# The compression's projections, blocks and first layer inside the loop of the recurrence

## The chip, the cores and the metric

The kernel runs on one core of a Trainium2 chip. A core has TensorE (matrix products, PE in the profile, with its weight loads as PEld), VectorE (DVE), ScalarE (ACT), GpSimd (POOL) and SyncE (SP, which here issues every DMA). Each engine takes its instructions in the order in which the program issues them. The metric is device microseconds of one execution.

## The reference

A decoder layer over 512 tokens of width 1024. After a norm, one wide product gives queries, keys and values of an attention, the input and gate of a recurrence (RG-LRU) and two merge gates. The parts that matter here are the compression of keys and values (blocks of 32 tokens through a two-layer network) and the recurrence:

```python
h = _rmsnorm(x, norm1_g)
proj = h @ w_in
# compression of keys and of values
blocks = jnp.concatenate([chunks[:, :-1], chunks[:, 1:]], axis=2) + pos[None, None, :, None, :]
hid = jax.nn.gelu(jnp.einsum('bnlgd,ldf->bngf', blocks, w1) + b1)
return jnp.einsum('bngf,fd->bngd', hid, w2) + b2
# recurrence
xc = conv(xb) + conv_b                       # 4 taps over time, per channel
r = sigmoid(xr @ wa + ba); i = sigmoid(xr @ wi + bi)   # 16 diagonal blocks
log_a = -LRU_C * r * softplus(-lam)
a = exp(log_a); b = sqrt(-expm1(2 * log_a)) * (i * xc)
h[t] = a[t] * h[t-1] + b[t]                  # scan over time
return h * gelu(gate)
```

Attention over compressed, selected and windowed keys follows, then the merge of both branches, an output product and a SwiGLU network with a residual.

## The kernel before

All products are float32 in three passes: each operand is split into a high half (float32r) and a low half (the rest), and `mm3` (L193) adds high by high, high by low and low by high. Weights come in the order of `weight_chunks` (L65) as chunks of 512 KB. `Weights.get(key, k, ahead)` (L174) hands out the next chunk after it has *cut* all chunks up to `ahead` further on, which are issued on ScalarE (the high half, L164) and VectorE (the low half, L167), and has issued the loads of two more on SP (L143). The raw chunks have two buffers, so a load waits until the chunk two before it has been cut. Cuts stand in the queues of ScalarE and VectorE where `get` is called: what is issued before them runs before them.

The recurrence's channels are 8 groups of 128. After the norm and the first group, the loop `for c in range(2, 8)` (L418) makes one turn for each group: the gate's projection of group c (`proj_cm`, 24 matmuls of 512 columns), `lru_coeffs(c-2)` (sigmoids and tanh on ScalarE, two operations on GpSimd, five products on VectorE), `lru_conv(c-1)` (a copy on ScalarE, the four taps on VectorE), the input's projection, `lru_parts(c-1)` (its split: `xch` on ScalarE, `xcl` on VectorE) and `lru_gates(c-1)` (six matmuls against diagonal blocks, which need both halves). The projections use four PSUM banks called dense, the gates two called s; two called t take transposes.

Behind the loop come, in this order: the four projections of the compression's keys and values, mixed with the rest of groups 6 and 7; `kv_evac` (four copies each that lay an accumulator out by pairs of tokens); and a loop over six of the sixteen merge gates (L550) that carries the rest. In this second loop stand the block additions `blocks_add` (GpSimd, L475), their split `blocks_split` (L186, L187), the first layer's eight weight chunks with 12 matmuls of 256 columns each (*hidden*), the roots `lru_roots` (ScalarE, L546), the product with the root and the scan `lru_scan` (GpSimd L379, VectorE L381), the gates' GELU (L575), `lru_out` (GpSimd L385 and a store), and at its end `hidden_gelu` (VectorE and ScalarE) and the memsets of the attention's tiles. In the second loop `get` is called with `ahead=2`. Key, query and value projections follow, where the halves of weights alternate between GpSimd and VectorE, then attention and the network.

The program's own list of what stands in a turn of the second loop:

```python
        for n in w1_after(c):
            kv, cc = divmod(n, 4)
            wh, wl = W.get(("w1", "cmp_w1_" + "kv"[kv], cc), 4, ahead=int(n in (7, w1_after(c)[-1])))
...
        W.cut(W.used + 1)
        W.load(W.used + 3)
        if c == 0:
            lru_roots(2, 4, 6)
```

Of the kernel before, what the change touches and what calls it, by code (L numbers as in the profile page):

```python
# [59 lines left out]
def w1_after(c):  # L60

    return [c] if c < 4 else [2 * c - 4, 2 * c - 3]


def weight_chunks():  # L65
# [34 lines left out]
def hybrid_block_kernel(ctx: ExitStack, tc: tile.TileContext, x: bass.AP, wpk: bass.AP,  # L100
# [257 lines left out]

    def lru_coeffs(c):
# [18 lines left out]
    def lru_scan(c):  # L378
        pool.tensor_tensor(out=tv[:, c, :], in0=tv[:, c, :], in1=mv[:, c, :], op=OP.mult)  # L379
        hs = live[c] = lt()  # L380
        dve.tensor_tensor_scan(hs, av[:, c, :], tv[:, c, :], 0.0, op0=OP.mult, op1=OP.add)  # L381

    def lru_out(c):
        lr = lt()
        pool.tensor_tensor(out=lr, in0=live.pop(c), in1=gg[:, c, :], op=OP.mult)  # L385
        nc.sync.dma_start(lru_d[c], lr)
# [31 lines left out]
    for c in range(2, 8):  # L418
        accg = proj_cm(cm("w_in", C_LRUG + P * c), ahead=1)
        lru_coeffs(c - 2)  # L420
        lru_conv(c - 1, accx)
        accx = proj_cm(cm("w_in", C_LRUX + P * c), ahead=1)
        lru_parts(c - 1)
        lru_gates(c - 1)
        act.copy(gg[:, c, :], accg)
        if c == 3:
            pool.iota(dm, pattern=[[-1, 512]], base=384, channel_multiplier=1,
                      allow_small_or_imprecise_dtypes=True)
            pool.iota(cd, pattern=[[P, NT], [-16, 32]], base=-31, channel_multiplier=1,
                      allow_small_or_imprecise_dtypes=True)  # L430
            pool.tensor_scalar(valid, cd[:, :, 0], 0.0, None, op0=OP.is_ge)
            for d in (dm, cd.rearrange("p t n -> p (t n)")):
                far = lt(n=d.shape[1])
                pool.tensor_scalar(far, d, 0.0, BIG, op0=OP.is_lt, op1=OP.mult)
                pool.tensor_tensor(out=d, in0=d, in1=far, op=OP.add)
# [13 lines left out]

    w2 = W.get(("w2",), 4, ahead=2)  # L450
    acck = [proj_cm(cm("w_in", 1024), ahead=2)]
    lru_conv(7, accx)
    lru_coeffs(6)
    lru_parts(7)
    acck.append(proj_cm(cm("w_in", 1024 + P), ahead=2))
    kv_evac(0, acck[0], act.copy)
    acck.append(proj_cm(cm("w_in", 1024 + 2 * P), ahead=2))
    lru_gates(7)
    lru_coeffs(7)
    kv_evac(1, acck[1], act.copy)  # L460

# [10 lines left out]
    def blocks_add(kv, v):  # L472
# [4 lines left out]
                           in1=pos[:, :, None, None].to_broadcast([P, 8, NKV, NCMP]), op=OP.add)  # L477

# [59 lines left out]
    blocks_add(0, 0)  # L538
    blocks_split(0, 0)
    blocks_add(0, 1)  # L540
    acck.append(proj_cm(cm("w_in", 1024 + 3 * P), ahead=2))
    kv_evac(2, acck[2], dve.tensor_copy)

    def lru_roots(*cs):
        for c in cs:
            act.activation(mv[:, c:c + 2, :], mv[:, c:c + 2, :], AF.Sqrt, scale=-4.0)  # L546

    lru_roots(0)
    acc = None
    for c in range(N_EARLY):  # L550
        prev, acc = acc, proj_cm(cm("w_in", C_MERGE + P * c), ahead=2)
        if c:
            merge_gate(c - 1, bc2, prev, bufs=1)
        if c == 0:
            kv_evac(3, acck[3], dve.tensor_copy)
            blocks_split(0, 1)
        if c in (2, 4):
            blocks_split(1, c // 2 - 1)
        for n in w1_after(c):
            kv, cc = divmod(n, 4)  # L560
            wh, wl = W.get(("w1", "cmp_w1_" + "kv"[kv], cc), 4, ahead=int(n in (7, w1_after(c)[-1])))
            if cc == 0:
                hid[kv] = bank("s")[:, :256]
            for jj in range(4):
                mm3(hid[kv], [m[:, 4 * (n % 2) + jj, :] for m in blk[kv, cc // 2]],
                    [w[:, jj, :] for w in (wh, wl)], cc == 0 and jj == 0, cc == 3 and jj == 3)
        W.cut(W.used + 1)
        W.load(W.used + 3)
        if c == 0:
            lru_roots(2, 4, 6)  # L570
        if c in (1, 3):
            blocks_add(1, c // 2)
        if c in (1, 2):
            for j in (4 * c - 4, 4 * c - 2):
                act.activation(gg[:, j:j + 2, :], gg[:, j:j + 2, :], AF.Gelu_apprx_tanh)  # L575
        if c > 1:
            lru_out(2 * c - 4)
            lru_out(2 * c - 3)
        if c < 4:
            lru_scan(2 * c)  # L580
            lru_scan(2 * c + 1)
        if c == 5:
            merge_gate(5, bc2, acc, bufs=1)
            hxt = bc.tile([P, 512], F32, tag="hx", name="hx", bufs=1)
            hxs = [hidden_gelu(kv, hid[kv]) for kv in range(2)]
            lru_es.close()
            vpool, v_es = open_pool(name="vpool", bufs=1)
            kpool, k_es = open_pool(name="kpool", bufs=16)
            vst = vpool.tile([P, 2, NT, NKV, P], F32R, name="vst")
# [4 lines left out]
            for m in (vcx, *kpad):  # L594
                pool.memset(f(m), 0.0)
# [699 lines left out]
```

## Time and profile before

| | us |
|---|---|
| median of 3 runs | 1012.44 (1012.0 to 1012.83) |
| the profiled execution | 1012.1 |
| its span, first to last instruction | 1010.0 |
| TensorE busy | 981.0 (97%) |
| VectorE busy | 570.5 (56%) |
| ScalarE busy | 458.6 (45%) |
| GpSimd busy | 223.1 (22%) |

The profile is one execution. Times in rows are microseconds from the start of the span unless marked ns. A busy share is an average over the whole span; the stretches of the region at hand say more. In rows of the timeline the first two numbers are the start and the duration, and what stands in brackets is how long the engine stood idle before the instruction and what ended it. A matmul's duration contains time that overlaps its neighbours, so that matmuls in a row are counted by their starts. Tile names are the program's: whi and wlo are the halves of a weight chunk, hth and htl those of the normed input, lt a tile of the recurrence's ring buffer, tv, av and mv its terms, decays and roots, shifted and blkh/blkl the compression's blocks.

### The profile page before, as it was taken

To read this page: it belongs to the slowest core of one execution; us is meant where nothing else is said; L and a number is where in the kernel's file an instruction comes from. 1 tells how busy PE (TensorE), PEld (TensorE's weight loads), DVE (VectorE), ACT (ScalarE), POOL (GpSimd) and SP (SyncE) were. 2 spreads that over 40 slices of the span, in tenths; PEclk is the share of its full clock that TensorE was granted. 3 is DMA by queue.
4 is the path that set the end of the run, shared out by engine and by line. 5 is a ranking of instruction groups with operands and counts; after the bars stand their busy time and mean duration, and the time that the engine had idled before them with its cause. 6 is when DMAs were issued, how large, how long until landed. Compare 5 with 4: busy or idle time off the path is not lost.

```text
span 1010.0 us, 13183 instructions
## 1 busy us (share of the span) xinstructions
PE 981.0 (97%) x4915; PEld 817.0 (81%) x4915; DVE 570.5 (56%) x1053; ACT 458.6 (45%) x867; POOL 223.1 (22%) x271
## 2 busy tenths in 40 slices
PE   6999997799999999999999999999999999999998
PEld 5878876588898888778888888988888888888887
DVE  5777679746766787887875544623322332231311
ACT  6544565336545777776773334523222322231210
POOL 1031148713201555645542002200000000000000
PEclk9999999999999999999999999999999999999999
DMA  5322324642213111322113464132332233232401
GB/s 190 105 84 83 123 84 138 196 148 92 90 56 116 63 53 43 105 84 64 33 63 99 151 254 132 45 122 84 88 119 86 83 92 117 84 125 63 167 21 42
DMA packets 32175, 100.65 MB, mean 100 GB/s; under 512 B 3696, under 2 KB 4080, under 8 KB 32112
## 3 DMA queue, kind: packets, MB, share of 16 engines
q1 hardware_dynamic: 32112, 99.82, 30.7%
q8 instruction: 38, 0.62, 0.2%
q14 instruction: 25, 0.20, 0.1%
HBM read 91.42 MB, written 8.39 MB: 99 GB/s over the span
## 4 chain that ended last, share of the span: by engine, by line
PE 86%; DVE 7%; ACT 3%; issue 2%; DMA 2%; POOL 0%; ACTq 0%; DVEq 0%
PE ps_b L197 14%; PE ps_b L198 14%; PE ps_b L196 14%; PE ps_dense L1006 9%; PE ps_dense L198 5%; PE ps_dense L197 5%; PE ps_dense L196 5%; PE ps_t L880 3%; PE ps_s L197 2%; PE ps_s L196 2%; PE ps_s L198 2%; DVE wlo L167 2%; PE ps_s L849 2%; PE ps_s L850 2%; PE ps_pv L908 2%
## 5 line engine op out<-in xcount | busy, mean ns | idle before, releaser
L167 DVE TENSOR_TENSOR wlo<-raw,whi 128x1024 fp32r<-128x1024 f32 (+2 forms) x199 | 193.6, 989 | 114.0 <-ACT whi L164 113.6
L164 ACT CAST whi<-raw 128x1024 fp32r<-128x1024 f32 (+2 forms) x207 | 166.0, 819 | 136.8 <-PE ps_b L198 69.1
L196 PE MATMUL ps_b<-h2h,whi 128*128 128x512 f32 (+1 forms) x376 | 143.4, 381 | 0.0
L198 PE MATMUL ps_b<-h2h,wlo 128*128 128x512 f32 (+1 forms) x376 | 143.2, 381 | 0.0
L197 PE MATMUL ps_b<-h2l,whi 128*128 128x512 f32 (+1 forms) x376 | 143.2, 381 | 0.0
L198 PE MATMUL ps_dense<-hth,wlo 128*128 128x512 f32 (+1 forms) x232 | 87.9, 379 | 11.2 <-DVE wlo L167 11.2
L871 POOL TENSOR_SCALAR p<-p,st,gates 128x128 f32<-128x128 f32 (+3 forms) x128 | 80.0, 638 | 84.7 <-DVE st L867 47.2
L1205 DVE TENSOR_TENSOR sg<-sg,ps_b 128x512 f32<-128x512 f32 x22 | 15.2, 689 | 138.2 <-PE ps_b L198 138.2
L196 PE MATMUL ps_dense<-hth,whi 128*128 128x512 f32 (+1 forms) x232 | 87.4, 377 | 0.0
L197 PE MATMUL ps_dense<-htl,whi 128*128 128x512 f32 (+1 forms) x232 | 87.1, 375 | 0.0
L197 PEld LDWEIGHTS ps_b<-h2l,whi 128*128 128x128 f32 x376 | 70.7, 188 | 15.0
L196 PEld LDWEIGHTS ps_b<-h2h,whi 128*128 128x128 f32 x376 | 70.7, 188 | 14.9
L198 PEld LDWEIGHTS ps_b<-h2h,wlo 128*128 128x128 f32 x376 | 70.7, 188 | 14.8
L861 ACT ACTIVATE p<-p,st 128x128 f32<-128x128 f32 (+3 forms) x128 | 72.0, 563 | 23.0 <-DVE st L856 22.3
L197 PE MATMUL ps_b<-wlo,gh 128*128 128x512 f32 (+1 forms) x198 | 73.2, 370 | 0.0
L198 PE MATMUL ps_b<-whi,gl 128*128 128x512 f32 (+1 forms) x198 | 73.1, 369 | 0.0
L196 PE MATMUL ps_b<-whi,gh 128*128 128x512 f32 (+1 forms) x198 | 73.1, 369 | 0.0
L186 ACT CAST gh<-sg 128x512 fp32r<-128x512 f32 x22 | 13.6, 620 | 123.2 <-DVE sg L1205 123.2
L892 DVE TENSOR_TENSOR ptl<-ps_t,pth 128x512 fp32r<-128x512 f32 x80 | 55.1, 689 | 21.1 <-ACT pth L886 20.4
L856 DVE CUSTOM_DVE_ANT_0 p<-ps_s,bias 128x128 f32<-128x128 f32 (+3 forms) x128 | 61.2, 482 | 9.2 <-PE ps_s L850 6.2
L198 PEld LDWEIGHTS ps_dense<-hth,wlo 128*128 128x128 f32 x232 | 44.4, 191 | 21.7 <-DVE wlo L167 13.5
L886 ACT CAST pth<-ps_t 128x512 fp32r<-128x512 f32 x80 | 46.5, 582 | 29.7 <-PE ps_t L880 29.2
(265 smaller groups left out, 2072.8 us busy)
## 6 DMA issues: line engine op xcount, KB each, us to landing
raw<-in_wpk_dram SPq DMA_DIRECT2D x150, 512.0 KB, 3.6
mg_d<-mt SPq DMA_DIRECT2D x16, 256.0 KB, 4.3
mt<-mg_d SPq DMA_DIRECT2D x16, 256.0 KB, 3.0
xt<-in_x_dram SPq DMA_DIRECT2D x4, 512.0 KB, 5.6
lru_d<-lt SPq DMA_DIRECT2D x8, 256.0 KB, 5.6
lraw<-lru_d SPq DMA_DIRECT2D x8, 256.0 KB, 2.7
x<-in_x_dram SPq DMA_DIRECT2D x4, 512.0 KB, 6.5
out_dram<-o SPq DMA_DIRECT2D x7, 256.0 KB, 2.0
```

Source lines behind the costliest of these rows:

```text
L164: (on_hi or act.copy)(hi[:, sl], raw[:, sl])
L167: eng.tensor_tensor(out=lo[:, sl], in0=raw[:, sl], in1=f(hi[:, sl]), op=OP.subtract)
L196: pe.matmul(acc, lhsT=ah, rhs=bh, start=start, stop=False)
L197: pe.matmul(acc, lhsT=ah, rhs=bl, start=False, stop=False)
L198: pe.matmul(acc, lhsT=al, rhs=bh, start=False, stop=stop)
L856: dve.tensor_tensor_reduce(out=p, in0=accs.pop((h, br, t)), in1=bias[h][:, 384 - t * P:512], scale=-1.0, scalar=3e38, op0=OP.add, op1=OP.m ...
L861: act.activation(p, p, AF.Exp, bias=stat[h][:, 0, br, t:t + 1], scale=-1.0, accum_out=stat[h][:, 1, br, t:t + 1])
L871: pool.tensor_scalar(p, p, sm[:, t:t + 1], gates[:, t, c:c + 1], op0=OP.mult, op1=OP.mult)
L880: pe.transpose(pt[:, o_:o_ + P], probs[h, br, t][:, k * P:(k + 1) * P], ident)
L886: act.copy(ph, pts[h, gi][0])
L892: dve.tensor_tensor(out=pl, in0=pt, in1=f(ph), op=OP.subtract)
L1006: pe.matmul(acc, lhsT=a[l], rhs=b[r], start=start and i == 0, stop=stop and i == 2)
```

## The change

The compression's four projections move into turns 2 to 5 of the first loop, behind the gates of the turn; their copies follow one turn later, all on ScalarE. The block additions stand in turns 4 to 7, their splits at the end of the same turns, and the first layer's eight chunks go by twos into turns 5, 6, 7 and behind the first merge projection. The weights' order in memory follows. The roots of groups 0 and 1 are taken in turn 4, of 2 and 3 in turn 6, the rest behind the loop, and the scans of groups 0, 1 and 2 stand in turns 5, 6 and 7; a scan's result goes over the roots instead of into the ring buffer. The rest of groups 6 and 7, five scans, the GELUs and the outputs are spread over the six merge projections, where `get` now has `ahead=1` and the extra cuts and loads are gone. The first layer's accumulators use the banks t instead of s. The pools of the compression open ahead of the loop.

```diff
-def w1_after(c):
-    return [c] if c < 4 else [2 * c - 4, 2 * c - 3]
+W1_AFTER = {5: (0, 1), 6: (2, 3), 7: (4, 5), 8: (6, 7)}
...
-    for c in range(2, 8):
-        L += [cm("w_in", C_LRUG + P * c), cm("w_in", C_LRUX + P * c)]
-    L += [("w2",)]
-    L += [cm("w_in", 1024 + P * c) for c in range(4)]
-    for c in range(N_EARLY):
+    for c in range(2, 9):
+        if c < 8:
+            L += [cm("w_in", C_LRUG + P * c), cm("w_in", C_LRUX + P * c)]
+        else:
+            L += [("w2",), cm("w_in", C_MERGE)]
+        if c < 6:
+            L += [cm("w_in", 1024 + P * (c - 2))]
+        L += [("w1", "cmp_w1_" + "kv"[j // 4], j % 4) for j in W1_AFTER.get(c, ())]
+    for c in range(1, N_EARLY):
         L += [cm("w_in", C_MERGE + P * c)]
-        L += [("w1", "cmp_w1_" + "kv"[j // 4], j % 4) for j in w1_after(c)]
...
     def lru_scan(c):
         pool.tensor_tensor(out=tv[:, c, :], in0=tv[:, c, :], in1=mv[:, c, :], op=OP.mult)
-        hs = live[c] = lt()
-        dve.tensor_tensor_scan(hs, av[:, c, :], tv[:, c, :], 0.0, op0=OP.mult, op1=OP.add)
+        dve.tensor_tensor_scan(mv[:, c, :], av[:, c, :], tv[:, c, :], 0.0, op0=OP.mult, op1=OP.add)
...
+    def hidden(n):
+        kv, cc = divmod(n, 4)
+        wh, wl = W.get(("w1", "cmp_w1_" + "kv"[kv], cc), 4, ahead=1)
+        if cc == 0:
+            hid[kv] = bank("t")[:, :256]
+        for jj in range(4):
+            mm3(hid[kv], [m[:, 4 * (n % 2) + jj, :] for m in blk[kv, cc // 2]],
+                [w[:, jj, :] for w in (wh, wl)], cc == 0 and jj == 0, cc == 3 and jj == 3)
...
     for c in range(2, 8):
         accg = proj_cm(cm("w_in", C_LRUG + P * c), ahead=1)
         lru_coeffs(c - 2)
         lru_conv(c - 1, accx)
+        if c in (4, 6):
+            lru_roots(c - 4)
+        if c >= 5:
+            lru_scan(c - 5)
         accx = proj_cm(cm("w_in", C_LRUX + P * c), ahead=1)
         lru_parts(c - 1)
+        if 3 <= c < 7:
+            kv_evac(c - 3, acck.pop(c - 3), act.copy)
         lru_gates(c - 1)
         act.copy(gg[:, c, :], accg)
+        if c >= 4:
+            blocks_add(*divmod(c - 4, 2))
+        if c < 6:
+            acck[c - 2] = proj_cm(cm("w_in", 1024 + P * (c - 2)), ahead=1)
+        for n in W1_AFTER.get(c, ()):
+            hidden(n)
+        if c >= 4:
+            blocks_split(*divmod(c - 4, 2))
...
+    w2 = W.get(("w2",), 4, ahead=1)
     acc = None
     for c in range(N_EARLY):
-        prev, acc = acc, proj_cm(cm("w_in", C_MERGE + P * c), ahead=2)
+        prev, acc = acc, proj_cm(cm("w_in", C_MERGE + P * c), ahead=1)
         if c:
             merge_gate(c - 1, bc2, prev, bufs=1)
         if c == 0:
-            kv_evac(3, acck[3], dve.tensor_copy)
-            blocks_split(0, 1)
...
-        W.cut(W.used + 1)
-        W.load(W.used + 3)
...
+            lru_conv(7, accx)
+            lru_coeffs(6)
+            lru_parts(7)
+            for n in W1_AFTER[8]:
+                hidden(n)
+        elif c == 1:
+            lru_gates(7)
+            lru_coeffs(7)
+            lru_scan(3)
+        elif c == 2:
+            lru_roots(4)
+            lru_roots(6)
+            lru_scan(4)
+            lru_scan(5)
+        elif c == 3:
+            for j in range(0, 8, 2):
                 act.activation(gg[:, j:j + 2, :], gg[:, j:j + 2, :], AF.Gelu_apprx_tanh)
+            lru_scan(6)
+            lru_scan(7)
             hxt = bc.tile([P, 512], F32, tag="hx", name="hx", bufs=1)
             hxs = [hidden_gelu(kv, hid[kv]) for kv in range(2)]
+        else:
+            for j in range(4 * c - 16, 4 * c - 12):
+                lru_out(j)
+    merge_gate(5, bc2, acc, bufs=1)
```

## Rows read from the trace of the kernel before

**Rows 1.** The page, 40 slices: TensorE's busy tenths and granted clock.
```profile
PE   6999997799999999999999999999999999999998
...
PEclk9999999999999999999999999999999999999999
```

**Rows 2.** Busy time by stretch: PE, PEld, DVE, ACT, POOL, clock, DMA share, GB/s.
```profile
40.00:113.00 73.00, 73.00 (x314) 58.54 (x313) 54.03 (x76) 35.05 (x53) 14.09 (x26) 1.00 0.24 76
...
148.00:205.00 57.00, 43.71 (x214) 35.56 (x215) 49.30 (x29) 28.21 (x31) 42.99 (x21) 0.97 0.57 169
```

**Rows 3.** TensorE's waits from 113 to 206: total us, times, longest.
```profile
PE ps_dense L198 <- DVE wlo L167: 10.8, 4, 5.1
PE ps_s L197 <- DVE wlo L167: 1.9, 1, 1.9
PE ps_dense L197 <- DVE wlo L167: 0.8, 1, 0.8
```

**Rows 4.** Timeline of TensorE, first loop and end of the second.
```profile
40.73 0.39 PE L196 MATMUL ps_dense<-hth,whi 128*128 128x512 f32 x1
...
51.93 0.39 PE L196 MATMUL ps_s<-lt,whi 128*128 128x512 f32 x1
...
198.16 0.28 PE L196 MATMUL ps_s<-whi,blkh 128*128 128x256 f32 x1
...
200.92 0.28 PE L198 MATMUL ps_s<-whi,blkl 128*128 128x256 f32 x1
```

**Rows 5.** Timeline of TensorE behind its longest wait.
```profile
160.86 0.80 PE L198 MATMUL ps_dense<-hth,wlo 128*128 128x512 f32 x1 [5.07 <-DVE wlo L167]
...
164.35 0.39 PE L197 MATMUL ps_dense<-htl,whi 128*128 128x512 f32 x1
```

**Rows 6.** Timeline of ScalarE, 100 to 145.
```profile
103.47 0.69 ACT L366 ACTIVATE lt<-ps_s,vec 128x512 f32<-128x512 f32 x1 [1.56 <-PE ps_s L198]
...
126.38 1.50 ACT L448 COPY kvp<-ps_dense 64x256 f32<-64x256 f32 x4
...
142.38 1.05 ACT L164 CAST whi<-raw 128x1024 fp32r<-128x1024 f32 x1
143.45 1.28 ACT L546 ACT_TABLE_LOAD   x1
```

**Rows 7.** Timeline of VectorE, one turn of the first loop.
```profile
100.87 0.69 DVE L187 TENSOR_TENSOR lt<-lt 128x512 fp32r<-128x512 f32 x1
...
106.23 0.69 DVE L372 TENSOR_TENSOR tv<-lt 128x512 f32<-128x512 f32 x1 [3.06 <-ACT lt L369]
...
110.07 2.33 DVE L344 SCALAR_TENSOR_TENSOR lt<-lt,vec 128x512 f32<-128x512 f32 x3
```

**Rows 8.** Loads of weight chunks (L143), 36 to 205.
```profile
DMA to landing us min/median/max: 3.1/3.5/5.4
```

**Rows 9.** SP's queue, 40 to 205: what its loads waited for, us, times, longest.
```profile
SPq L143 <- DVE wlo L167: 128.6, 30, 11.5
```

**Rows 10.** Timeline of VectorE beside GpSimd.
```profile
139.04 2.90 DVE L375 SCALAR_TENSOR_TENSOR av<-mv,lt 128x512 f32<-128x512 f32 x1
...
151.83 1.21 DVE L167 TENSOR_TENSOR wlo<-raw,whi 128x1024 fp32r<-128x1024 f32 x1
152.97 5.69 DVE L381 TENSOR_TENSOR_SCAN lt<-av,tv 128x512 f32<-128x512 f32 x2
```

**Rows 11.** Timeline of GpSimd beside it.
```profile
138.43 2.96 POOL L475 TENSOR_TENSOR shifted<-kvp,vec 128x992 f32<-128x992 f32 x1 [1.25 <-ACT kvp L448]
...
151.99 3.44 POOL L475 TENSOR_TENSOR shifted<-kvp,vec 128x992 f32<-128x992 f32 x1 [1.16 <-DVE blkl L187]
155.38 4.34 POOL L379 TENSOR_TENSOR tv<-tv,mv 128x512 f32<-128x512 f32 x2
```

**Rows 12.** Timeline of VectorE, the two GELUs of the first layer.
```profile
205.41 0.42 DVE L486 TENSOR_TENSOR hx<-ps_s,rowt 128x256 f32<-128x256 f32 x1
...
210.12 0.43 DVE L491 SCALAR_TENSOR_TENSOR hx<-hu,hx 128x256 f32<-128x256 f32 x1 [0.55 <-ACT hu L490]
```

More of the change, by code (lines that the diff above doesn't have):

```diff
@@ L417, in hybrid_block_kernel @@
     act.copy(gg[:, 1, :], acc3[2])
[L418 to L435, printed above, removed]
     xa_es.close()
@@ L537, in hybrid_block_kernel @@
     hid = [None, None]
[L538 to L548, printed above, removed]
+    acck = {}
+    for c in range(2, 8):
+        accg = proj_cm(cm("w_in", C_LRUG + P * c), ahead=1)
+        lru_coeffs(c - 2)
+        lru_conv(c - 1, accx)
+        if c in (4, 6):
+            lru_roots(c - 4)
+        if c >= 5:
+            lru_scan(c - 5)
+        accx = proj_cm(cm("w_in", C_LRUX + P * c), ahead=1)
+        lru_parts(c - 1)
+        if 3 <= c < 7:
+            kv_evac(c - 3, acck.pop(c - 3), act.copy)
+        lru_gates(c - 1)
+        act.copy(gg[:, c, :], accg)
+        if c >= 4:
[6 more added lines that the diff above has]
+            blocks_split(*divmod(c - 4, 2))
+        if c == 3:
+            pool.iota(dm, pattern=[[-1, 512]], base=384, channel_multiplier=1,
+                      allow_small_or_imprecise_dtypes=True)
+            pool.iota(cd, pattern=[[P, NT], [-16, 32]], base=-31, channel_multiplier=1,
+                      allow_small_or_imprecise_dtypes=True)
+            pool.tensor_scalar(valid, cd[:, :, 0], 0.0, None, op0=OP.is_ge)
+            for d in (dm, cd.rearrange("p t n -> p (t n)")):
+                far = lt(n=d.shape[1])
+                pool.tensor_scalar(far, d, 0.0, BIG, op0=OP.is_lt, op1=OP.mult)
+                pool.tensor_tensor(out=d, in0=d, in1=far, op=OP.add)
+    w2 = W.get(("w2",), 4, ahead=1)
     acc = None
     for c in range(N_EARLY):
-        prev, acc = acc, proj_cm(cm("w_in", C_MERGE + P * c), ahead=2)
+        prev, acc = acc, proj_cm(cm("w_in", C_MERGE + P * c), ahead=1)
         if c:
@@ L592, in hybrid_block_kernel @@
-            gates = vpool.tile([P, NT, 48], F32, name="gates")
-            gcmp = vpool.tile([P, NT, NH], F32, name="gcmp")
-            for m in (vcx, *kpad):
-                pool.memset(f(m), 0.0)
+        else:
+            for j in range(4 * c - 16, 4 * c - 12):
+                lru_out(j)
+    merge_gate(5, bc2, acc, bufs=1)
+    lru_es.close()
+    vpool, v_es = open_pool(name="vpool", bufs=1)
+    kpool, k_es = open_pool(name="kpool", bufs=16)
+    vst = vpool.tile([P, 2, NT, NKV, P], F32R, name="vst")
@@ L596, in hybrid_block_kernel @@
+    vcx = vpool.tile([P, NH, P], F32R, name="vcx")
+    kpad = [vpool.tile([P, 96 + NKV * P], F32R, name=f"kpad{i}") for i in range(2)]
+    gates = vpool.tile([P, NT, 48], F32, name="gates")
+    gcmp = vpool.tile([P, NT, NH], F32, name="gcmp")
+    for m in (vcx, *kpad):
+        pool.memset(f(m), 0.0)
     bc2_es.close()
```

45 lines of the change are left out of this document (3 added, 42 removed).

## The prediction

> **What bounds the kernel now.** I read the page first: TensorE is busy in nearly every slice at the full granted clock, with one dip between slices 5 and 8 [rows 1]. The stretches say where: from 148 to 205 us TensorE is busy 43.7 of 57 us, while VectorE is busy 49.3 and GpSimd 43.0 [rows 2]. The waits there have one cause, five long ones and one short: TensorE stands before the low half of a weight chunk that VectorE has not yet cut [rows 3]. So this region is a contest between TensorE's work, which the change keeps matmul for matmul, and the rate at which chunks are cut.
>
> First, what can be won. A projection is 24 matmuls; 48 of them lie between 40.73 and 51.93, so 5.6 us each, 0.233 a matmul, and six gate matmuls take 1.4. A first-layer chunk ("hidden") is 12 matmuls; the last two of them run from 198.16 to 201.04, 1.44 each [rows 4]. From the loop's first matmul at 40.73 to the last hidden matmul, which ends at 201.04, stand 22 projections (12 of the recurrence, 4 of the compression, 6 merge gates), 7 gates and 8 hiddens: 123.2 + 9.7 + 11.5 = 144.4 us, and they take 160.3. So 15.9 us are lost, of which about 1.5 is matmuls at the lower of the two clock levels, 1.2 GHz for 2.4, behind the longest wait (eight take 3.5 us and not 1.9) [rows 5]. The first key chunk loses another 1.0 (its 0.8 wait and the restart) [rows 3]. All stalls gone would be 16.9 us; I work out what the new order loses instead.
>
> **Prices.** On ScalarE a high half takes 1.05, the four sigmoids and tanhs of a turn 2.75 until VectorE's first product can start (103.47 to 106.23), the four copies of a compression accumulator 1.5, a table load 1.28 [rows 6, 7]. On VectorE the coefficients and the convolution take 6.1 (106.23 to 112.40), the low half 1.14 from one start to the next, the recurrence's own low part (xcl) 0.6 [rows 7]. A load lands 3.5 us after its issue in the median, between 3.1 and 5.4 [rows 8]; there are two raw buffers, so the load of a chunk starts when the chunk two before it has its low half, which is what the queue waits for [rows 9]. From a low half's end to the high half of the chunk two later I take 3.55.
>
> The decisive price is GpSimd against VectorE. The block add on GpSimd starts at 138.43 and ends at 141.39, and VectorE's 0.69 us operation takes 2.90 beside it: GpSimd had it from 139.01 on, 2.4 us [rows 10, 11]. The third add behaves so too: the low half that started before it is not slowed (1.21), the scan behind it starts at 152.97 and the pair ends 5.69 later. Taking turns, add until 155.43, scan, product (GpSimd's L379), scan, fits 158.66 with a scan at 1.1 and the product at 1.05 [rows 10, 11]. Nothing in the trace shows a scan without GpSimd: 1.1 is an estimate from these rows, its bounds 0.7 (a plain 512-wide operation) and 2.85 (half the pair). I take each GpSimd add or product that falls into VectorE's chain as 2.4 or 1.05 on top.
>
> **The change, part by part.** Moved into the loop are four projections and their 16 copies (ScalarE; two sets of four leave VectorE, which saves nothing on the path as it comes after the loop), four adds and splits, six of eight hiddens, roots of channels 0 to 3, three scans with their GpSimd products. The scans write over the roots instead of a ring buffer: no cost, the buffer ring only gets freer. The row-vector load and the memset move ahead of the loop, where SP and GpSimd have no late work. Two root calls inside the loop and two after it make seven table loads of three: four more, 5.1 us of ScalarE, hidden where ScalarE idles, but not in turn 7 (below). After the loop the look-ahead falls from two chunks to one.
>
> Turns 2 to 4 gain 5.6 us of TensorE cover each for 1.14 of VectorE and lose nothing. Put zero at the end of turn 4's gates. TensorE, unstalled: compression projection to 5.6, two projections to 16.8, gates(4) to 18.2, projection and two hiddens to 26.7, two projections to 37.9, gates(5) to 39.3, hiddens 42.2, two projections 53.4, gates(6) 54.8, hiddens 57.7, first merge projection 63.3, hiddens 66.2, second 71.8, gates(7) 73.2, four more to 95.6.
>
> Turn 5: ScalarE starts at 0.15, the first product at 2.9; coefficients and convolution with one product and one add of GpSimd inside: +6.1+3.45 = 12.45; scan 13.55; low half 14.7; xcl 15.35. Gates(4) wait for nothing. Then chunks: ScalarE comes to the first w1 chunk at 15.1 (after split and copies), low half 17.3; the second waits for its load, 14.7+3.55, low half 20.45; the next gate chunk 17.3+3.55, low 23.1; the next x chunk 20.45+3.55, high 25.05, low 26.2. Two more chunks a turn, each pair a load, a high and a low apart: that is where the look-ahead goes.
>
> Turn 6: its sigmoids, ready since 18.2, stand behind that high half in ScalarE's queue and start at 25.05; first product 27.8; +6.1+1.05 = 34.95; scan 36.05; low 37.2; here the next add comes in, to 39.6; xcl 40.2. Gates(5) end at 41.45, 2.15 late. Second w1 chunk's low 41.35; the x chunk's load lands at 44.9, high 45.95; a table load, as the roots came between, 47.25.
>
> Turn 7: sigmoids 47.25, product 50.0, +6.1+3.45 = 59.55, scan, low half, xcl 62.4. Gates(6) end at 63.65 against 54.8: 8.85 lost so far. One turn of this chain has taken 22.2, TensorE's takes 15.5.
>
> After the loop: the first merge chunk loads only after 63.55, is cut at 69.4, TensorE had been ready for it at 66.55 and two matmuls more: 2.35. Behind it stand one low half, convolution and coefficients (6.1), xcl and the last low half, from 70.6 to 80.1 with 0.4 that I allow for GpSimd's two small operations of that turn; the last hidden was due at 76: 4.1. The fourth merge chunk: gates(7) end at 88.5; sigmoids 2.9, coefficients 3.25, product and scan 2.15, low half 1.15 until 97.95, wanted at 94.6: 3.4. Then four scans and products, one low half, and the two hidden GELUs at 2.6 each (205.41 to 210.55) [rows 12] until 111.8, high and low half until 113.5; TensorE wanted it at 109.2: 4.3. The sum: 8.85+2.35+4.1+3.4+4.3 = 23.0. Half-speed matmuls as in [rows 5] behind waits of four us and more: those behind gates(6) are covered by the next wait; behind the last hidden and the last merge chunk 0 to 1.5 each; I take 1.6 in all. The first key chunk no longer waits. GpSimd now does its eight output products and the memsets late, until about 121, and then cuts a key chunk which is due at 124: 0, bound 2. SP's queue has the eight output stores in those two projections too, ahead of the third key chunk's load, which is wanted after 124.
>
> So 1012.1 (this execution, 1010.0 of it the span) - 16.9 + 23.0 + 1.6 = 1019.8. The median of the runs shown is 1012.44, a third of a microsecond above it; I say 1020.
>
> Against splitting the roots speaks a rule of the Trainium skill ("ScalarE: Activation LUTs", Table sets: the hidden batching unit): batch activations by table set, since a switch costs the load and a drain, about 2.66 us. Here the cast ahead of a load ends at 143.43, the load starts at 143.45 and takes 1.28 [rows 6]; with the page's price turn 7 would be 1.4 longer and the sum 1021.
>
> **The rivals.** *GpSimd fits into gaps* (0.14): where VectorE waits for sigmoids and loads, adds and products would cost the chain nothing. Redoing the sum without them: gates(4) to (6) lose nothing, then 1.8, 3.6, 2.4 and 1.2, together 9.0, so 1012.1 - 16.9 + 9.0 = 1004. This is the one on the other side; it decides once over 6.1 of the 14 us between the sums fall away (23.0 to 16.9). For it: VectorE has idle time in the loop, 3.06 ahead of one product alone [rows 7]. Against it: GpSimd's product and add are queued right behind its own work of the same turn, so they start with VectorE's chain, not before. The Trainium skill ("SBUF — State Buffer", Who interferes with whom) says the port pair of the two is held for a whole instruction, which this trace bears out at 2.90 for 0.69; by it this rival is unlikely.
> *Everything hides* (0.06): the cuts keep up, 995 to 1002. For it: VectorE is busy 54.0 of 73 us in the loop's old form [rows 2]; against it, the pair of raw buffers, whose loads wait for VectorE [rows 9].
> *About half of the GpSimd cost* (0.10): 1010 to 1014.5, half of that within the bound of no change.
> *Heavier* (0.13): loads land later than 3.5, towards the 5.4 that some take beside stores [rows 8]. One us on each of the six load waits on the chain is 6: 1024 to 1031.
> *The forecast* (0.57): 1014.5 to 1024.
>
> **The numbers.** Within 0.2% (about 2 us, what a measurement of this kernel can tell from none) 0.05, faster 0.25, slower 0.70. 1005 to 1026 leaves out some 0.1 below and 0.07 above; the forecast's own range is 1014.5 to 1024.
>
> **What would show it.** After: gates(6) waiting six to nine us on VectorE's xcl (the weight of one recurrence turn), ScalarE idle before high halves on loads in turns 6 and 7, waits before the first merge chunk, the last hidden, the fourth and the sixth merge chunk; no dip before turn 6; GpSimd's adds beside stretched convolutions. Wrong it would be if the chain in turn 5 ends well before 15, if ScalarE reaches turn 6's sigmoids by 18 to 20 and not 25, or if VectorE's operations beside GpSimd's are not longer than alone.

## The result, and the profile after

The change makes the kernel slower: 1035.61 us (1034.15 to 1037.43) against 1012.61 (1012.0 to 1012.83) on the same chip, a ratio of 1.023, interval 1.0217 to 1.0242. The forecast had the sign; of the size it had 7.4 us where 23.0 came, and the time lies above the range. The profiled execution has a span of 1034.1 against 1010.0.

On the page TensorE's dip, once between slices 5 and 8 of before [rows 1], begins one slice earlier and the granted clock dips for three slices:

```profile
PE   6999977879999999989999999999999999999998
...
PEclk9999998889999999999999999999999999999999
```

By stretch, in the columns of [rows 2] (the loop's first turns, then three short stretches around the longest waits): the first 73 us are no longer full, and in the three TensorE is granted 0.60 to 0.67 of its clock.

```profile
40.00:113.00 73.00, 71.12 (x303) 56.56 (x302) 47.99 (x59) 37.51 (x56) 18.69 (x22) 1.00 0.27 89
...
150.00:161.00 11.00, 3.77 (x10) 2.78 (x11) 9.51 (x13) 3.40 (x5) 0.46 (x2) 0.67 0.12 26
...
195.00:203.30 8.30, 8.07 (x23) 6.36 (x24) 8.27 (x8) 3.34 (x4) 3.46 (x2) 0.61 0.47 140
...
214.00:224.00 10.00, 9.02 (x24) 6.66 (x25) 3.28 (x2) 2.00 (x3) 3.96 (x4) 0.60 0.70 205
```

TensorE's waits from 40 to 245, total, times and longest, which answer to [rows 3]:

```profile
PE ps_s L198 <- ACT lt L188: 6.6, 3, 5.9
PE ps_dense L200 <- DVE wlo L169: 6.4, 3, 4.9
PE ps_dense L198 <- ACT whi L166: 5.0, 1, 5.0
PE ps_s L199 <- DVE lt L189: 4.5, 4, 1.7
PE ps_t L199 <- DVE wlo L169: 3.5, 2, 3.0
PE ps_dense L199 <- POOL wlo L169: 1.5, 1, 1.5
```

They sum to 27.5 us, where before had 13.5. Three are new in kind: gates that wait for ScalarE's and VectorE's halves of the recurrence's input (L188, L189), a chunk that waits for its high half, and a key chunk that waits for GpSimd's low half. The places where the waits are long, from TensorE's timeline:

```profile
155.83 0.80 PE L198 MATMUL ps_s<-lt,whi 128*128 128x512 f32 x1 [5.88 <-ACT lt L188]
158.03 0.80 PE L199 MATMUL ps_s<-lt,whi 128*128 128x512 f32 x1 [1.41 <-DVE lt L189]
...
175.65 0.39 PE L199 MATMUL ps_t<-wlo,blkh 128*128 128x256 f32 x1 [3.01 <-DVE wlo L169]
...
195.22 0.79 PE L200 MATMUL ps_dense<-hth,wlo 128*128 128x512 f32 x1 [4.94 <-DVE wlo L169]
...
214.02 0.80 PE L198 MATMUL ps_dense<-hth,whi 128*128 128x512 f32 x1 [5.00 <-ACT whi L166]
```

These are gates(6), the last hidden, the fourth merge chunk and the sixth. Against TensorE's work without stalls (the prediction's 144.4 us from the loop's first matmul) the region up to the end of the sixth merge chunk loses 38.7 us, and the first key chunk 1.8 more, together 40.5 where before lost 16.9. That is 23.6 of the 24.1 us between the spans; of the 40.5, waits are 27.5 and matmuls at the lower clock level and restarts 13.0.

What stands behind gates(6), first on ScalarE and then on VectorE:

```profile
59.08 1.05 ACT L166 CAST whi<-raw 128x1024 fp32r<-128x1024 f32 x1 [7.61 <-PE ps_dense L199]
...
90.07 1.05 ACT L166 CAST whi<-raw 128x1024 fp32r<-128x1024 f32 x1 [2.78 <-PE ps_dense L199]
...
93.04 1.28 ACT L371 ACT_TABLE_LOAD   x1
94.33 0.69 ACT L371 ACTIVATE lt<-ps_s,vec 128x512 f32<-128x512 f32 x1
...
117.94 1.05 ACT L166 CAST whi<-raw 128x1024 fp32r<-128x1024 f32 x1 [4.79 <-PE ps_t L200]
...
120.79 0.68 ACT L371 ACTIVATE lt<-ps_s,vec 128x512 f32<-128x512 f32 x1
...
141.65 1.28 ACT L371 ACT_TABLE_LOAD   x1
142.94 0.69 ACT L371 ACTIVATE lt<-ps_s,vec 128x512 f32<-128x512 f32 x1
...
155.16 0.62 ACT L188 CAST lt<-lt 128x512 fp32r<-128x512 f32 x1 [8.07 <-DVE lt L346]
```
```profile
145.70 0.69 DVE L377 TENSOR_TENSOR tv<-lt 128x512 f32<-128x512 f32 x1 [2.81 <-ACT lt L374]
...
148.13 2.84 DVE L379 SCALAR_TENSOR_TENSOR lt<-lt 128x512 f32<-128x512 f32 x1
...
155.04 1.22 DVE L385 TENSOR_TENSOR_SCAN mv<-av,tv 128x512 f32<-128x512 f32 x1
156.18 1.20 DVE L169 TENSOR_TENSOR wlo<-raw,whi 128x1024 fp32r<-128x1024 f32 x1
157.29 0.68 DVE L189 TENSOR_TENSOR lt<-lt 128x512 fp32r<-128x512 f32 x1
```

The rows from 141.65 on are the chain that the prediction forecast for turn 7 (behind load and high half the table load, sigmoids, coefficients beside GpSimd, scan, low half, xcl). The last row's end lets gates(6) go on. What it did not have are the high halves that wait for TensorE, for 7.61, 2.78 and 4.79 us; behind the second of them stand turn 5's sigmoids (94.33), behind the third turn 6's (120.79).

### The profile page after: what moved, and what is told of

Same layout as the page of the kernel before. It is cut to its first block, busy times and chain, and to the rows that moved or that the text cites. A ratio compares the mean times of both kernels' runs of the same rounds, so it can differ in the third digit from the quotient of the medians.

```text
span 1034.1 us, 13173 instructions
## 1 busy us (share of the span) xinstructions
PE 989.8 (96%) x4915; PEld 821.8 (79%) x4915; DVE 564.6 (55%) x1044; ACT 466.1 (45%) x879; POOL 215.7 (21%) x272
## 4 chain that ended last, share of the span: by engine, by line
PE 80%; DVE 9%; ACT 6%; DMA 3%; issue 2%; POOL 0%; SPq 0%; ACTq 0%; DVEq 0%
PE ps_b L200 13%; PE ps_b L199 13%; PE ps_b L198 13%; PE ps_dense L1005 9%; PE ps_dense L199 4%; PE ps_dense L200 3%; PE ps_dense L198 3%; PE ps_t L879 3%; PE ps_s L199 2%; PE ps_s L200 2%; PE ps_s L198 2%; PE ps_s L848 2%; PE ps_s L849 2%; PE ps_pv L907 2%; PE ps_pv L906 2%
## 5 line engine op out<-in xcount | busy, mean ns | idle before, releaser
L169 DVE TENSOR_TENSOR wlo<-raw,whi 128x1024 fp32r<-128x1024 f32 (+2 forms) x198 | 190.2, 977 | 140.8 <-ACT whi L166 140.3
L860 ACT ACTIVATE p<-p,st 128x128 f32<-128x128 f32 (+3 forms) x128 | 72.0, 563 | 23.6 <-DVE st L855 22.9
L188 ACT CAST gh<-sg 128x512 fp32r<-128x512 f32 x22 | 13.6, 620 | 123.2 <-DVE sg L1204 123.2
L885 ACT CAST pth<-ps_t 128x512 fp32r<-128x512 f32 x80 | 46.5, 582 | 29.8 <-PE ps_t L879 29.3
```

Of the source, the lines that this page charges most:

```text
L169: eng.tensor_tensor(out=lo[:, sl], in0=raw[:, sl], in1=f(hi[:, sl]), op=OP.subtract)
L860: act.activation(p, p, AF.Exp, bias=stat[h][:, 0, br, t:t + 1], scale=-1.0, accum_out=stat[h][:, 1, br, t:t + 1])
L885: act.copy(ph, pts[h, gi][0])
```

## The experiments

All ratios are to the kernel before, on the same chip in the same session, with 95% intervals; "lt" is the recurrence's ring buffer. Most intervals reach about 1.5 us to either side, so that a difference of one or two microseconds between versions is not clear of noise.

**A cycle of three weight buffers.** The halves of chunk i go to buffer pool i mod 5 of (stage2, stage, stage, stage2, stage). The two diagonal weights are chunks 3 and 4 and keep their buffers up to the last gates: one of stage2's two and one of stage's three. So of each five chunks the first and the one two before it share what is left of stage2, and a high half waits until TensorE is through a chunk that is only two back.

```diff
-    W.stage(five, (stage2,), (dve,))
+    W.stage((stage2, stage, stage), (stage2,), (dve,))
```

> The changed kernel, with the halves of the weight chunks in another order of buffers: one of the small stage and two of the large in a cycle of three, and not of five, up to the key chunks; no memory is added. Theory A (the two diagonal weights hold one buffer in each stage for the whole loop, so that every fifth cut waits until TensorE is through the chunk two before it): ScalarE's waits for TensorE ahead of high halves (7.6 at 59 us, 2.8 at 90, 4.8 at 118, 2.3 at 163) go, the sigmoids of turn 6 start at about 115 and not at 120.8, gates(6) end some 5 us earlier, and the time is 1028 to 1032. Rival: raw buffers and GpSimd set that pace anyway, and the time stays within 1.5 us of 1035.6.

Measured: 1032.86 us, ratio 1.0196 (1.0181 to 1.0211), 2.8 less than with the change alone. Gates(2) and (4) lose nothing, and the gates(6) end at 156.02 instead of 160.33, 4.3 earlier. But the same wait stands in front of them, and the sixth merge chunk waits 6.16 and not 5.00:

```profile
PE ps_dense L198 <- ACT whi L166: 6.2, 1, 6.2
PE ps_s L198 <- ACT lt L188: 5.9, 1, 5.9
```

So the buffers cost 4.3 us at gates(6), and 2.8 in the end. Not all waits for a buffer are gone, as the theory had it: with three, a chunk's halves need those of the chunk three back. ScalarE then waits 10.5 us in six waits, where it waited 17.5 in four, and ahead of turn 6's sigmoids still 3.98 for 4.79:

```profile
113.69 1.05 ACT L166 CAST whi<-raw 128x1024 fp32r<-128x1024 f32 x1 [3.98 <-PE ps_dense L199]
...
116.54 0.68 ACT L371 ACTIVATE lt<-ps_s,vec 128x512 f32<-128x512 f32 x1
```

**The merge gates in the ring.** In the change's second loop a merge gate's tile has one buffer, and the third gate cannot be written before the store of the second is done, which stands in SP's queue behind a load. ScalarE, after the change alone:

```profile
199.92 1.28 ACT L438 ACT_TABLE_LOAD   x1 [7.61 <-DMA mg_d<-mt]
```
```profile
195.20 0.33 SPq L145 DMA_DIRECT2D raw<-in_wpk_dram  x1
195.59 0.42 SPq L439 DMA_DIRECT2D mg_d<-mt  x1
```
```diff
-        mt = pool_.tile([P, T], F32, tag="mt", name="mt", **kw)
+        mt = pool_.tile([P, T], F32, tag="mt", name="mt", **kw) if pool_ else lt()
...
-            merge_gate(c - 1, bc2, prev, bufs=1)
+            merge_gate(c - 1, None, prev)
```

> The changed kernel, with the merge gates of the second loop in the recurrence's ring buffer and not in one tile of their own, so that a gate need not wait for the store of the one before. Theory B (the store stands in SP's queue behind a load that waits for a raw buffer, ScalarE's third gate waits for the store for 7.6 us, and GELUs, first layer and the sixth merge chunk wait for ScalarE): this wait is gone, the 5.0 and 1.0 us waits for the sixth merge chunk shrink to 2 or less and its half-speed matmuls go with them; 1026 to 1030. Rival: GpSimd's outputs and the hidden GELUs on VectorE take its place, 1033 to 1035.

Measured: 1034.05, ratio 1.0212 (1.0197 to 1.0227). The 7.61 are gone from ScalarE, and the sixth chunk still waits 5.72: what stood behind the store's wait waits for scans and outputs instead. The time is 1.6 less, with an interval that overlaps that of the change. Both edits together:

> The cycle of three buffers and the gates in the ring buffer together. If A and B act in different places, the sum of both: 1021 to 1025; if the second only moves the wait that the first leaves, no better than the better of the two by more than 2 us.

Measured: 1030.13, ratio 1.0176 (1.0161 to 1.0191). Together they save 5.5 us, which the noise does not tell from 2.8 and 1.6 apart; fourth and sixth chunk wait 4.97 and 6.91.

**The block additions cut to one column.** GpSimd's four additions of 992 columns are cut to 32.

```diff
-        pool.tensor_tensor(out=shifted[:, :, :, :NCMP], ...
+        pool.tensor_tensor(out=shifted[:, :, :, :1], ...
```

> The changed kernel with the block additions cut to one of 31 columns (the rest of the blocks is left at zero: part of the computation is left out). Theory C (each add blocks VectorE for 2.4 us in the chain of turns 5, 6 and 7): gates(4) to gates(6) come 1, 2 and 5 us or more earlier, 1027 to 1031. Rival: the chain waits for the halves' buffers, and what the adds free is lost there again: 1033 to 1036.

Measured: 1031.84, ratio 1.019 (1.0173 to 1.0207). Gates(4) lose nothing, gates(6) wait 2.47 and 1.70 instead of 5.88 and 1.41. The gates(6) end 4.3 earlier; three additions on that chain at the 2.4 of the forecast would be 7.2. So about 0.6 of the forecast price was found there, and 3.8 us of the total come back.

**TensorE kept busy.** Sixteen idle matmuls stand ahead of gates(6), of the fourth and of the sixth merge chunk.

```diff
+    def idle_mm(acc, n=16):
+        for _ in range(n):
+            pe.matmul(acc, lhsT=hT[0][0][:, :P], rhs=hT[0][0], start=True, stop=True)
...
+        if c == 6:
+            idle_mm(pr)
...
+        if c in (3, 5):
...
+            idle_mm(acc)
```

> The changed kernel with 16 extra matmuls of the normed input by itself ahead of gates(6), of the fourth and of the sixth merge projection, into the bank that is written next (3.7 us of work of no use, where TensorE waits 5.9, 4.9 and 5.0 us). Theory D (the half-speed matmuls behind these three waits are a cost of their own, some 2.7, 2.9 and 3.1 us): the granted clock stays at full and the time falls by all of it, to 1026 to 1028. Rival: what TensorE gains behind one wait it loses in the next, which VectorE and ScalarE set, and only the last one counts, 1031 to 1033.

Measured: 1036.8, ratio 1.0241 (1.0226 to 1.0257). The granted clock from 140 to 245 us goes from 0.87 to 0.92, and the waits shrink in the timeline:

```profile
155.85 0.50 PE L198 MATMUL ps_s<-lt,whi 128*128 128x512 f32 x1 [2.06 <-ACT lt L188]
...
196.88 0.50 PE L200 MATMUL ps_dense<-hth,wlo 128*128 128x512 f32 x1 [1.38 <-DVE wlo L169]
...
216.20 0.79 PE L198 MATMUL ps_dense<-hth,whi 128*128 128x512 f32 x1 [4.68 <-ACT whi L166]
```

The clock stayed up only behind the fourth chunk (1.00 from 196 to 202): the last matmuls of gates(6) and the first of the sixth chunk are still 0.43 apart, and the second merge chunk is newly slow (0.51 from 177.2 to 180.4), which makes gates(7) 1.6 later. The starts do not come earlier: 155.85 for 155.83, and 196.88 and 216.20 are later than 195.22 and 214.02. From the start of the third merge chunk, right behind gates(7), to where the fourth goes on it is 11.2 us in both runs, and from there to the sixth's start 19.3 for 18.8. So without the slow stretch behind the fourth chunk, the sixth is no sooner ready; for the other two places the run does not show it.

**Look-ahead of two in the second loop**, on the version with three buffers and the ring.

```diff
-        wh, wl = W.get(("w1", "cmp_w1_" + "kv"[kv], cc), 4, ahead=1)
+        wh, wl = W.get(("w1", "cmp_w1_" + "kv"[kv], cc), 4, ahead=1 + int(n > 5))
...
-    w2 = W.get(("w2",), 4, ahead=1)
+    w2 = W.get(("w2",), 4, ahead=2)
...
-        prev, acc = acc, proj_cm(cm("w_in", C_MERGE + P * c), ahead=1)
+        prev, acc = acc, proj_cm(cm("w_in", C_MERGE + P * c), ahead=2)
```

> The cycle of three and the gates in the ring buffer as before, and a look-ahead of two chunks again from the second layer's weights on. Theory E (the fourth and sixth merge chunk wait since only one chunk is cut ahead of what VectorE does between two cuts): their waits of 5.0 and 6.9 us fall to 2 or less together, 1019 to 1023 against 1030.1 of that kernel. Rival: VectorE and GpSimd have more work there than TensorE covers, the waits move by a chunk, and no more than 3 us are won.

Measured: 1026.94, ratio 1.0141 (1.0126 to 1.0156), 3.2 less than without. The fourth chunk's wait falls from 4.97 to 0.40 and the last hidden's goes, but the second chunk now waits 2.54 and 2.24, and the sixth 7.45.

**The hidden GELUs behind the sixth merge gate.**

```diff
         elif c == 3:
-            hxs = [hidden_gelu(kv, hid[kv]) for kv in range(2)]
...
     merge_gate(5, bc2, acc, bufs=1)
+    hxs = [hidden_gelu(kv, hid[kv]) for kv in range(2)]
```

> The changed kernel with the first layer's two GELUs behind the sixth merge gate and not in the fourth merge projection. If their place ahead of the sixth chunk's cut makes its wait (GELUs stand in VectorE's and ScalarE's queue for 10 us there), the wait of 5.0 and 1.0 us goes with its half-speed matmuls: 1026 to 1029, and the key projections wait for nothing new. Rival: ScalarE's wait for the store of a gate (7.6 us) keeps it there: 1033 to 1036.

Measured: 1034.39, ratio 1.0217 (1.0202 to 1.0233). The sixth chunk's 5.00 become 0.54; the key chunks behind it wait 1.96, 2.13 and 1.93. Of 5 us moved, 1.2 are saved, with an interval that overlaps that of the change.

**The first layer out of the loop.** Its eight chunks and the values' blocks go back into the second loop as in the kernel before, with its look-ahead of two, and the two hidden GELUs stand behind the sixth merge gate; projections, keys' blocks, roots and three scans stay in the first loop, with three buffers and the ring.

```diff
-        L += [("w1", "cmp_w1_" + "kv"[j // 4], j % 4) for j in W1_AFTER.get(c, ())]
...
-        for n in W1_AFTER.get(c, ()):
-            hidden(n)
...
     for c in range(N_EARLY):
+        for n in w1_after(c):
+            hidden(n)
```

> One part of the change undone: the first layer's eight chunks and the values' blocks stand in the second loop as in the kernel before, with its look-ahead of two, so that turns 6 and 7 have two chunks; the projections, the keys' blocks, the roots and the three scans stay in the first loop (cycle of three, gates in the ring buffer). If four chunks a turn stretch the chain of the recurrence (a pair of loads, high and low halves each), gates(5) and gates(6) wait for 1 us or less together and the second loop, with three scans and products less than before, loses less than the 15.9 us of the kernel before: 1004 to 1010. Rival: the adds and scans alone stretch turns 5 to 7, 1013 to 1020.

Measured: 1014.79 (10 runs), ratio 1.0023 (1.0013 to 1.0032). Against the version with three buffers and the ring that is 15.3 us, and with those two edits 20.8 of the change's 23.0 are regained. The gates(6) wait 0.23 and 0.90 and end at 140.46; one long wait is left, behind the last coefficients and scan(3):

```profile
171.52 0.79 PE L199 MATMUL ps_dense<-hth,wlo 128*128 128x512 f32 x1 [6.91 <-DVE wlo L168]
```

**Two projections only**, the keys' in turns 2 and 3, on that version; the values' two stand behind the loop as in the kernel before, and with them the rest of groups 6 and 7; the second loop's roots, scans, GELUs and outputs come a merge chunk or two earlier.

> The version without the first layer in the loop of the recurrence (1014.8), but with only the keys' two projections in turns 2 and 3; the values' two stand behind the loop again, as in the kernel before, where they cover the last convolution, coefficients and gates. My theory (what costs is how much stands in one turn beside the recurrence, and the loss at the third merge gate there is the missing cover behind the last gates): the 6.9 us wait ahead of the fourth merge chunk shrinks below 3, gates(6) and gates(7) still lose 1 to 2, total 1005 to 1011, below the kernel before. Rival (the scans and roots in the loop are what keeps that version from gaining, wherever the projections stand): 1013 to 1016.

Measured: 1022.09, ratio 1.0096 (1.0082 to 1.011): 7.3 us slower than that version, where the theory had it faster and the rival the same. The fourth chunk's wait fell to 3.28, but gates in the loop now wait 4.17 (gates(4)) and 1.12 (gates(6)), gates(7) 2.71. My theory named the wrong place: as far as these waits show, the projections in turns 4 and 5 had been the cover of the scans. How much of the 7.3 us is due to what moved in the second loop, no run separates.

**The scans alone**, in the kernel before: roots of groups 0 to 3 and scans 0 to 2 in the first loop.

```diff
         lru_conv(c - 1, accx)
+        if c in (4, 6):
+            lru_roots(c - 4)
+        if c >= 5:
+            lru_scan(c - 5)
```

> The kernel before with one part of the change alone: the roots of channels 0 to 3 and the scans 0 to 2 in the loop of the recurrence, nothing else moved. Theory (the scans behind the gates fill idle time of VectorE in three-chunk turns, and four scans fewer follow the loop): the waits in the merge chunks, where three scans stood, shrink by 2 to 4 us, and the turns lose under 1.5: 1008 to 1012. Rival (a scan of 1.1 in each of turns 5 to 7 stands on VectorE's chain ahead of the low halves, and the two further table loads in ScalarE's): turns 6 and 7 lose 1.5 to 3 each more than they did, 1013 to 1017.

Measured: 1016.81, ratio 1.0043 (1.0031 to 1.0056): the rival's time, though turn 6 loses nothing. Gates(4) and gates(6) wait, and behind the first of these, short as they are, TensorE falls to the lower level (granted clock 0.50 from 94 to 96 us):

```profile
92.83 0.49 PE L197 MATMUL ps_s<-lt,whi 128*128 128x512 f32 x1 [1.70 <-DVE lt L187]
...
94.47 0.63 PE L196 MATMUL ps_dense<-hth,whi 128*128 128x512 f32 x1
94.89 0.63 PE L197 MATMUL ps_dense<-htl,whi 128*128 128x512 f32 x1
```

**No loads for the first layer**, on the version with three buffers and the ring.

```diff
+                if keys[i][0] == "w1":
+                    self.raw[i] = gg[:, 0:2, :].rearrange("p a t -> p (a t)")
+                    self.loaded += 1
+                    continue
```

> The change with the cycle of three weight buffers and the merge gates in the ring (1030.1), where the eight chunks of the first layer are not loaded: their halves are cut from a tile that is in SBUF already (the gates' branch of two channels), with the same casts, subtractions and matmuls. The loads of w1 are left out. Theory (the pair of raw buffers and the landing of 3.5 us after a low half set the pace of the turns of four chunks): the wait ahead of gates(6), 5.85 + 1.41 with the loads, falls to under 2.5, that of the last hidden to under 2, and the time to 1017 to 1024. Rival (the cuts themselves, a high half of 1.05 and a low half of 1.14 for each of two more chunks a turn, and the chain through sigmoids, products and convolution set it): the wait stays at 5 or more, the time at 1027 to 1030.

Measured: 1024.51, ratio 1.0119 (1.0105 to 1.0133), 5.6 less, half a microsecond outside the theory's range. The wait ahead of gates(6) falls by 3.0, from 5.73 and 1.41 to 2.41 and 1.71, where the theory asked for 4.8 or more. That of the last hidden stays at 3.0, and both long waits of the second loop stay too:

```profile
PE ps_dense L202 <- ACT whi L170: 7.0, 1, 7.0
PE ps_dense L204 <- DVE wlo L173: 5.0, 1, 5.0
```

**Neither loads nor additions:**

> The change with three weight buffers and the ring (1030.1), without w1's loads (halves cut from a tile in SBUF) and with GpSimd's four block adds cut to one of 31 columns: both are left out. Theory (loads and adds are two parts of one chain on VectorE and ScalarE, and their shares add up): the wait ahead of gates(6), 5.7 + 1.4, falls to under 1.5, that is by 3.0 for the loads and 3.4 for the adds, and the time to 1017 to 1022. Rival (they hide behind each other, or the two more cuts a turn keep the chain as long): the wait stays at 3 or more, 1022 to 1025.

Measured: 1022.7, ratio 1.0099 (1.0083 to 1.0114). The wait is 0.50 and 1.70, so the two take 4.9 of its 7.1: more than either alone, less than their sum of 6.1 (3.1 was the additions' share on the change itself). In time the additions give only 1.8 more, which is the rival's figure and not clear of noise: fourth and sixth chunk wait 4.96 and 6.74 as ever.

**Three buffers in the kernel before:**

> The kernel before with one line changed: its weight halves go round a cycle of three buffers instead of five, so that no high half waits for the two buffers that the diagonal weights hold. Theory (the waits of ScalarE's high halves for TensorE, 2.78 and 1.51 there, cost something in the kernel before too): its five waits of TensorE in the loop shrink by 2 to 4 us together, 1008.5 to 1011. Rival (before the last two gates TensorE waits for VectorE's coefficients and low halves, not for a high half, so a buffer more changes nothing): 1012 to 1013.

Measured: 1012.03 (11 runs), ratio 0.9996 (0.9987 to 1.0005), no difference. ScalarE waited for TensorE there too (4.3 us in two waits), but those waits were not on the path: with three buffers they are gone, and the time is the same.

**The projections beside the scans.** One each at the end of turns 4, 5 and 6, the fourth behind gates(7), the first layer outside:

```diff
-        if c < 6:
-            acck[c - 2] = proj_cm(cm("w_in", 1024 + P * (c - 2)), ahead=1)
+        if 4 <= c < 7:
+            acck[c - 4] = proj_cm(cm("w_in", 1024 + P * (c - 4)), ahead=1)
...
+        if c == 1:
+            acck[3] = proj_cm(cm("w_in", 1024 + 3 * P), ahead=1)
```

> The version without the first layer in the loop (1014.8), with the same four projections placed elsewhere: one each at the end of turns 4, 5 and 6, so that each scan of turns 5 to 7 has 5.6 us of TensorE in front of its gates, and the fourth behind the last gates, where 6.9 us were lost ahead of the fourth merge chunk. Theory (each turn with a scan needs a third projection as cover, each turn without one does not): gates(4) to gates(6) lose nothing, the wait of 6.9 falls below 2, total 1004 to 1011, below the kernel before. Rival (the scans, GpSimd's products and the outputs behind the gates take the gain back at the later merge chunks and the first key chunk): 1012 to 1016.

Measured: 1015.19, ratio 1.0024 (1.0014 to 1.0034), no better than the version it was made from. The loop behaves as the theory has it: gates(4) to gates(6) lose nothing. The second loop takes it back:

```profile
170.81 0.79 PE L201 MATMUL ps_dense<-hth,wlo 128*128 128x512 f32 x1 [6.11 <-DVE wlo L170]
...
191.56 0.58 PE L200 MATMUL ps_t<-wlo,blkh 128*128 128x256 f32 x1 [5.26 <-DVE wlo L170]
```

**The projections without the scans in the loop:**

> The version without the first layer in the loop (1014.8), where the roots and all eight scans stand behind the loop as in the kernel before; the four projections and the keys' blocks stay in the loop. Theory (under the cover of the projections the scans of turns 5 and 6 cost nothing, and behind the loop they stretch the low halves beside GpSimd's products): slower than with the scans in the loop, 1016 to 1022. Rival (scans on VectorE's chain cost in the loop too, as they did alone, +4.5): 1010 to 1014.

Measured: 1015.51, ratio 1.0028 (1.0016 to 1.0039), between what the two theories gave. Its interval overlaps that of the version with the scans: under the projections' cover no cost and no gain can be told. No gates of the loop wait, and the fourth merge chunk, which waited 6.91 with them, waits 7.13 for its high half and 2.82 for its low half.

No version beat the kernel before. A third raw buffer, which would show how much the pair of them costs without leaving a load out, was not tried.

## Why the prediction missed the size

**The step that failed** is "Turns 2 to 4 gain 5.6 us of TensorE cover each for 1.14 of VectorE and lose nothing", with the zero that the sum sets at the end of turn 4's gates and "ScalarE starts at 0.15" behind it. It counted ScalarE's and VectorE's work and the loads, and left out that a high half needs a free weight buffer. The trace of before has such waits (ScalarE's 4.3 us in two), and a third chunk in a turn makes more of them: 7.61 ahead of turn 3's sigmoids, behind which gates(2) wait 1.1, and 2.78 ahead of turn 5's. The zero is 91.48 in the trace of after, and turns 2 to 4 have lost 1.5 there. Turn 5's sigmoids start at 94.33, which is 2.85 on the forecast's clock and not 0.15; a table load of 1.28 stands ahead of them, which the sum put at nothing. Turn 6's start at 29.3 and not 25.05, turn 7's at 51.5 and not 47.25, and the loss at the end of gates(6) is 15.7 and not 8.85. From turn 6's sigmoids to turn 7's the chain takes 22.15, where the forecast had 22.2: the error lay ahead of it. In the run with three buffers turns 2 to 4 lose nothing, the zero is at 89.94, turn 6's sigmoids start at 26.6 on that clock, and 4.3 of the 6.85 come back at gates(6), which shows the cause. In the time it is 2.8 of the 15.8 us between the sum's 1019.8 and 1035.6; the rest stands in the terms below. Of the 2.5 that are left, 1.1 is that the gates behind xcl run at the lower clock level (2.36 from xcl's end to theirs, where the forecast had 1.25); the rest are waits for a buffer and the table load, which no run separates.

**The mechanism was right.** Four chunks and more in a turn are more than ScalarE, VectorE and two raw buffers cut in the time of TensorE's work: the version with the first layer outside shows 15.3 us for it, of which the look-ahead of two that goes with it gave 3.2 when it was tried alone; the GELUs' place, 1.2 on the change, goes with it too. In that chain, additions and loads were both at work, 4.9 of 7.1 us at gates(6). The durations that were bounded held: a scan without GpSimd takes 1.14 from start to start (155.04 to 156.18; the estimate was 1.1), and VectorE's 0.69 operation takes 2.84 beside the addition (2.90 in [rows 10]). That bears out again what the Trainium skill says of the port pair ("SBUF — State Buffer", Who interferes with whom): one of the two has it for a whole instruction. The table load at 141.65 costs 1.28, and the sigmoid starts as it ends. The Trainium skill's dearer switch ("ScalarE: Activation LUTs", What ACT_TABLE_LOAD costs: load and drain, about 2.66 us) is thus not seen here, as the prediction took it.

**Terms that were mis-sized.** First merge chunk 0.35 (forecast 2.35), last hidden 3.5 (4.1), fourth chunk 8.0 (3.4), sixth 9.6 (4.3), key chunk on GpSimd 1.8 (0, bound 2). In fourth and sixth 4.94 and 5.96 are waits, and the rest is 14 and 15 matmuls at the lower level, 0.43 us apart and not 0.233 [rows 4]; behind gates(6) two hiddens take 4.43 instead of 2.88. Slow matmuls and restarts are 13.0 of the 40.5 in all, where 1.6 was allowed: of all terms this one is the furthest off. At the fourth chunk they are not a price that one could save by itself, as the idle matmuls show there: the chain on ScalarE and VectorE sets when the next chunk is ready. At the other places that is argued, not shown.

**What the terms hid** is that they are not a sum. Three buffers gained 4.3 at gates(6) and 2.8 in the end, the ring 7.6 on ScalarE and 1.6, late GELUs 4.5 at the sixth chunk and 1.2; the 1.6 and the 1.2 are within the noise. In the second loop everything that VectorE, GpSimd and ScalarE have to do behind the last gates stands ahead of the fourth and the sixth merge chunk, and the waits there (about 5 and 5 to 7 us) stay in nearly every version that carries the first layer in the loop. With look-ahead two the fourth's goes and the sixth's grows.

**The rivals.** That everything hides is false, and that GpSimd fits into gaps too, since cutting the additions gave 3.8 us back. The rival of half the GpSimd cost was nearest on that one price (4.3 of 7.2 at gates(6)), and still 21 us off in time, as the other terms grew. The rival of heavier loads came nearest in time, and they were not the cause; the median is that of before [rows 8]:

```profile
DMA to landing us min/median/max: 2.1/3.5/5.8
```

Part by part, as far as runs show: the scans alone +4.5; projections and keys' blocks, with three buffers and the ring, +3.2, with the scans +2.4; the first layer's chunks in the loop, with the values' blocks, the GELUs' place and a look-ahead of one, 15.3 more; the buffers and the store that this makes matter, 5.5 more. The steps 2.4, 15.3 and 5.5 lead from the kernel before to the change, so they have to add up to its 23.0 but for noise (23.2); that they do says nothing for the parts inside each.

## What to carry to other kernels

Before weights are moved into a loop, write down for each chunk not only who cuts it but which buffer its halves need and which matmul frees it; weights that stay for a whole loop make the ring shorter for all others. A loop that one engine fills has room for a chunk a turn only if every other engine of the chain from load to split has it too, and a gain at one wait is worth what is left of it at the next one. Work moved under cover costs nothing there and gains nothing either, if the place that it left waits for something else.

## What the hardware showed that I had not expected

TensorE fell to the lower of its two levels behind waits of only 0.21 and 1.70 us: in the run with the scans alone matmuls stand 0.43 apart from 93.63 on, and the granted clock from 94 to 96 is 0.50. The changed kernel has the same two waits ahead of gates(5), with the same distance between them, and keeps the full clock (1.00 from 134 to 136):

```profile
131.51 0.51 PE L198 MATMUL ps_s<-lt,whi 128*128 128x512 f32 x1 [0.22 <-ACT lt L188]
133.71 0.50 PE L199 MATMUL ps_s<-lt,whi 128*128 128x512 f32 x1 [1.70 <-DVE lt L189]
134.05 0.39 PE L200 MATMUL ps_s<-lt,wlo 128*128 128x512 f32 x1
```

Nor did its wait of 3.01 ahead of the last hidden bring the level down (1.00 from 177 to 180), while behind the same wait in the run with idle matmuls the second merge chunk ran at 0.51. So a wait of up to three microseconds did not by its length say here whether the clock would fall. Behind its two waits of 5 us, 14 and 15 matmuls ran at the lower level.
